# Down products of two SwiGLU blocks: seven block products in place of the plain product, with their sums formed on POOL and kept in DRAM

## The chip, the cores and the metric

The kernel runs on one core of a Trainium2 chip. The metric is the device time of one execution in microseconds (us). Engines: PE multiplies matrices, DVE, ACT and POOL work on elements, and SP issues the DMAs. Each engine has an in-order queue; the order in it is set when the program is built, by a list scheduler of the framework that the kernel is written in.

## The reference

One step of a one-layer streaming encoder on 1024 prompt rows and 64 sample rows of width 1024, in float32, with D_FF = 2816:

```python
def swiglu(x, w_gate, w_up, w_down):
    return (jax.nn.silu(x @ w_gate) * (x @ w_up)) @ w_down

def macaron_half(x, g, b, w_gate, w_up, w_down):
    return layer_norm(ALPHA * x + 0.5 * swiglu(x, w_gate, w_up, w_down), g, b)
```

The layer is `macaron_half`, then a mixer (input projection, sparse attention with an indexer in one group of heads, forgetting attention in the other, output projection, layer norm), then a second `macaron_half`. Keys and values of the new rows are outputs too.

## The kernel before

Each float32 operand is split into a high part (a cast to fp32r on ACT) and a low part (the rest, by a subtraction on DVE; `split`, L106 to L108). A product is then three matmuls of 128x512: high by high, high by low, low by high (`mm`, L111).

**Gate and up** (`ffn_a`). The hidden rows are taken in two halves, j and j + 11, with j from 0 to 10, and the tokens in two halves of 512, so that each of the two weights and the tokens are 2x2 blocks. A body (j, u), u = 0 for gate and 1 for up, forms the block of the product by seven block products (Strassen and Winograd). Its weight sums S1 to S4 come from four POOL operations (L323), with a cast (L326) and a split (L327) of each; its token sums T1 to T4 are formed once, in the stage's start (`finish`), by POOL and DVE. The first product that reads a sum is fy, T2 by S2. The stage's start, j = 0, works without S sums. After body (j, 1) `times` forms the hidden block on DVE (L247) and `emit_h` writes its four blocks of 128x512 to DRAM (L241). The blocks live in a ring of tiles. Gate and up weights are loaded two bodies ahead (`raw_of`, L411).

**Down** (`ffn_b`, `gemm_b`). Plain: three groups of three token tiles, 22 k-steps each. A k-step loads 128x1024 of `w_down` (L202) and the tokens of the group (L487), splits both, and multiplies: eight token tiles need 3 matmuls for each 512 columns, and the ninth tile, the 64 sample rows with their low parts beside them, needs 2. The weights are read three times. Then come residual, layer norm (`layer_norm`, L499 to L519) and the turned operand for the next stage.

The order of the kernel is `ffn_a` and `ffn_b` of the first block, the mixer, the output projection, and `ffn_a` and `ffn_b` of the second block. All loads and stores go through SP's queue. Names that the rows use: gb for the accumulators of the down product, fa, fy, fz and fs for those of gate and up, wst for a raw weight tile, ringz0 and ringz1 for tiles of the ring, zz for residual rows, hd for the hidden blocks in DRAM.

Of the kernel before, what the change touches and what calls it, by code (L numbers as in the profile page):

```python
# [18 lines left out]
P = 128  # L19
# [27 lines left out]
def hybrid_step(ctx: ExitStack, tc: tile.TileContext, i, o):  # L47
# [70 lines left out]

    def turned(t, z, hf):
        r = rows_of(t)  # L120
        pt = sm(f"xt{t}_{hf}")
# [92 lines left out]
    def ffn_a(xo, wg, wu, hd, during, tags, pre=()):  # L214
# [153 lines left out]
        def sample(j, pss):  # L368
# [12 lines left out]
            for b in range(2):  # L381
                DMA.dma_start(hd[j + b * NJ][:, SEQ:TT], hs[:, b * DEC:(b + 1) * DEC])
# [112 lines left out]
    def layer_norm(t, z, acc, gt, bt):  # L495
# [6 lines left out]
        yield  # L502
        st = sp.tile([P, 2, 6], F32, tag="bst", name="bst")
# [60 lines left out]

    def ffn_b(hd, wd, gn, bn, res, emit, last=False):
        with tc.tile_pool(name="hb", bufs=1) as hb_:
            st = {}

            def room(late):
                if late == 0:  # L570
                    st["room"] = hb_.tile([P, 4, 2, 1024], F32R, tag="room", name="room")
                return st["room"][:, late, 0, :], st["room"][:, late, 1, :]

            gemm_b(NF, h_split(hd, st), wd, zz_pre(st, res, gn, bn), zz_post(st, emit), 1, 4, room, last)

    hd1 = [dp.tile([P, TT], F32, name=f"hd1_{k}") for k in range(NF)]
    hd2 = [dp.tile([P, TT], F32, name=f"hd2_{k}") for k in range(NF)]
# [104 lines left out]
    with tc.tile_pool(name="xe", bufs=1) as xe:  # L682
        xo = Strassen(xe)
        ring_of(xo, ("z1",))
        wg1, wu1 = w2("ffn1_w_gate"), w2("ffn1_w_up")
        ffn_a(xo, wg1, wu1, hd1, cgen, ("z0",), load_x(xo, wg1, wu1))
# [17 lines left out]
    ap_ = tc.tile_pool(name="att", bufs=1)  # L704
# [21 lines left out]
    pin_ = tc.tile_pool(name="pin", bufs=1)  # L726
# [77 lines left out]
    def in_proj(gi, tiles=range(NT), ahead=2):  # L804
# [3 lines left out]
        for t in tiles:  # L808
# [10 lines left out]
            pump((0, 0, 3, 3, 0, 0, 0, 0, 0)[t] if gi == 0 else 3)  # L819
# [50 lines left out]
    pidx_ = tc.tile_pool(name="pidx", bufs=1)  # L870
# [351 lines left out]
    in_proj(0, range(2, 6))  # L1222
    cached_kidx()
    in_proj(1, range(6), -1)
    pump_all()
    in_proj(0, range(6, NT), -1)
    in_proj(1, range(6, NT), 7)
# [10 lines left out]
    pc_ = tc.tile_pool(name="pc", bufs=2)  # L1238
# [348 lines left out]
    pf_ = tc.tile_pool(name="pf", bufs=2)  # L1587
# [30 lines left out]
    xe_ = tc.tile_pool(name="xe2", bufs=1)  # L1618
# [27 lines left out]
    ffn_a(xo2[0], w2("ffn2_w_gate"), w2("ffn2_w_up"), hd2, iter(()), ("z1", "z0"))  # L1646
# [58 lines left out]
```

## Time and profile before

| | |
|---|---|
| median of 3 runs | 2414.56 us (2414.2 to 2414.74) |
| profiled execution, its own time | 2413.24 us |
| its span | 2411.5 us |
| PE busy | 2275.1 us (94%), 11999 matmuls |
| DVE busy | 1571.4 us (65%) |
| ACT busy | 1058.9 us (44%) |
| POOL busy | 743.3 us (31%) |
| DMA | 316.4 MB, 131 GB/s on average |
| chain that ended last | PE 76%, DVE 14%, DMA 3%, issue 3%, ACT 3%, POOL 1% |

The stages lie, in us of the span, at 0 to 519 (gate and up, first block), 519 to 792 (down), 792 to 1535 (mixer), 1535 to 1640 (output projection), 1640 to 2137 (gate and up, second block, with its start to 1705) and 2137 to the end (down). A share over the whole span mixes them, so the windows of a stage say more. A wait is named by what ended it. PEclk is the granted share of PE's full clock.

### The profile page before, as it was taken

To read this page: it belongs to the slowest core of one execution; us is meant where nothing else is said; L and a number is where in the kernel's file an instruction comes from. 1 tells how busy PE (TensorE), PEld (TensorE's weight loads), DVE (VectorE), ACT (ScalarE), POOL (GpSimd) and SP (SyncE) were. 2 spreads that over 40 slices of the span, in tenths; PEclk is the share of its full clock that TensorE was granted. 3 is DMA by queue.
4 is the path that set the end of the run, shared out by engine and by line. 5 is a ranking of instruction groups with operands and counts; after the bars stand their busy time and mean duration, and the time that the engine had idled before them with its cause. 6 is when DMAs were issued, how large, how long until landed. Compare 5 with 4: busy or idle time off the path is not lost.

```text
span 2411.5 us, 34602 instructions
## 1 busy us (share of the span) xinstructions
PE 2275.1 (94%) x11999; PEld 1936.8 (80%) x11999; DVE 1571.4 (65%) x2680; ACT 1058.9 (44%) x1999; POOL 743.3 (31%) x1018
## 2 busy tenths in 40 slices
PE   8899999999999999887778999999899999999997
PEld 6788888888887999787667887788688888888885
DVE  7555465544665545999988777588754655545665
ACT  4333333333444356664556788633333333333432
POOL 4322232200001434225367677503432322200010
PEclk9999999999999999998878999999999999999999
DMA  4444432256666344243366741553132222265673
GB/s 156 141 140 133 121 91 64 80 175 191 198 196 213 102 133 148 76 135 101 92 149 152 189 115 43 166 187 111 56 95 63 89 64 80 80 204 169 211 225 113
DMA packets 293625, 316.42 MB, mean 131 GB/s; under 512 B 41326, under 2 KB 241454, under 8 KB 293450
## 3 DMA queue, kind: packets, MB, share of 16 engines
q1 hardware_dynamic: 293450, 314.20, 43.3%
q8 instruction: 95, 1.56, 0.3%
q14 instruction: 80, 0.66, 0.1%
HBM read 235.54 MB, written 78.58 MB: 130 GB/s over the span
## 4 chain that ended last, share of the span: by engine, by line
PE 76%; DVE 14%; DMA 3%; issue 3%; ACT 3%; POOL 1%; SPq 0%; DVEq 0%; POOLq 0%; ACTq 0%
PE fa L111 20%; PE gb L111 16%; PE fz L111 9%; PE fy L111 5%; PE ip L111 5%; DVE s L984 4%; PE gb_a L111 4%; PE gb_b L111 4%; PE fs L111 3%; PE pq L111 2%; PE acc L111 2%; PE pt L1406 2%; PE iq L111 1%; PE xt L124 1%; DMA wst<-ffn_w_down 1%
## 5 line engine op out<-in xcount | busy, mean ns | idle before, releaser
L107 ACT CAST wh<-wst 128x1024 fp32r<-128x1024 f32 x232 | 244.0, 1052 | 348.8 <-PE fs L111 144.5
L108 DVE TENSOR_TENSOR wl<-wst,wh 128x1024 fp32r<-128x1024 f32 x232 | 294.5, 1270 | 133.8 <-ACT wh L107 130.3
L326 ACT CAST Sh<-S 128x512 fp32r<-128x512 f32 x160 | 97.0, 619 | 238.8 <-PE fa L111 148.8
L323 POOL TENSOR_TENSOR S<-wst 128x512 f32<-128x512 f32 x80 | 109.4, 1368 | 273.4 <-DVE Sl L327 147.5
L490 POOL CAST hh<-hl 128x64 fp32r<-128x64 f32 x36 | 19.6, 545 | 537.9 <-DVE hl L108 528.2
L327 DVE TENSOR_TENSOR Sl<-S,Sh 128x512 fp32r<-128x512 f32 x160 | 150.5, 944 | 23.7 <-ACT Sh L326 22.5
L111 PE MATMUL gb<-wh,hh 128*128 128x512 f32 x480 | 154.3, 392 | 5.8 <-ACT hh L107 5.8
L323 POOL TENSOR_TENSOR S<-wst,S 128x512 f32<-128x512 f32 x40 | 72.0, 1799 | 249.5 <-issue 155.6
L107 ACT CAST hh<-hr 128x384 fp32r<-128x384 f32 (+1 forms) x120 | 59.7, 497 | 200.3 <-PE gb_b L111 167.2
L111 PE MATMUL gb<-wl,hh 128*128 128x512 f32 x480 | 146.1, 389 | 0.0
L108 DVE TENSOR_TENSOR hl<-hr,hh 128x384 fp32r<-128x384 f32 (+1 forms) x120 | 64.3, 535 | 124.1 <-ACT hh L107 114.3
L111 PE MATMUL gb<-wh,hl 128*128 128x512 f32 x480 | 140.4, 389 | 0.0
L111 PE MATMUL acc<-pp,vs 128*128 128x256 f32 (+1 forms) x640 | 122.9, 311 | 7.2 <-DVE pp L108 5.0
L108 DVE TENSOR_TENSOR pp<-pt,pp 128x512 fp32r<-128x512 f32 (+1 forms) x160 | 98.0, 630 | 21.0 <-ACT pp L107 20.4
L1362 POOL TENSOR_SCALAR e<-e,su 128x128 f32<-128x128 f32 (+7 forms) x128 | 99.8, 791 | 33.7 <-DVE su L1359 17.8
L111 PEld LDWEIGHTS gb<-wh,hh 128*128 128x128 f32 x480 | 89.0, 188 | 25.4 <-ACT hh L107 7.5
L111 PE MATMUL ip<-wh,xh 128*128 128x256 f32 x368 | 107.6, 292 | 1.7 <-DVE lt L659 1.6
L111 PEld LDWEIGHTS acc<-pp,vs 128*128 128x128 f32 x640 | 96.9, 204 | 14.9 <-DVE pp L108 8.6
L1406 PE MATMUL pt<-ident,e 128*128 128x128 f32 x576 | 99.8, 294 | 9.2 <-POOL e L1362 8.5
L991 ACT ACTIVATE csum<-s,neg 128x1024 f16<-128x1024 f32 (+1 forms) x62 | 72.9, 1175 | 80.7 <-DVE neg L988 77.8
L111 PE MATMUL ip<-wh,xl 128*128 128x256 f32 x368 | 105.6, 287 | 0.0
L111 PE MATMUL ip<-wl,xh 128*128 128x256 f32 x368 | 105.5, 287 | 0.0
(496 smaller groups left out, 7028.0 us busy)
## 6 DMA issues: line engine op xcount, KB each, us to landing
wst<-ffn_w_down SPq DMA_DIRECT2D x132, 512.0 KB
wst<-ffn_w_gate SPq DMA_DIRECT2D x88, 256.0 KB
wst<-ffn_w_up SPq DMA_DIRECT2D x88, 256.0 KB
hd<-ringz SPq DMA_DIRECT2D x88, 256.0 KB
hr<-hd SPq DMA_DIRECT2D x88, 192.0 KB
wst<-w_out SPq DMA_DIRECT2D x24, 512.0 KB
hr<-hd SPq DMA_DIRECT2D x44, 160.0 KB
wst<-w_in SPq DMA_DIRECT2D x12, 512.0 KB
```

The source lines that it names most:

```text
L107: S.copy(hi, src)
L108: V.tensor_tensor(lo, src, f(hi), ALU.subtract)
L111: PE.matmul(out, lhsT, rhs, start=start, stop=stop, skip_group_check=more)
L124: PE.transpose(pt[:, q * r:(q + 1) * r], z[:r, k * P:(k + 1) * P], ident[:r, :r])
L323: G.tensor_tensor(t, ss[0] if x is None else x, ss[1] if y is None else y, op)
L326: S.copy(hi, t)
L327: V.tensor_tensor(lo, t, f(hi), ALU.subtract)
L490: G.tensor_copy(hh[:, 320:384], f(hl[:, 256:320]))
L984: V.tensor_scalar(junk.bitcast(src.dtype)[:, :n], src[:, of:of + n], th[:, e:e + 1], None, op, ALU.add, accum_out=out[:, e:e + 1])
L991: S.activation(csum[:, :n], sc[b], AF.Sign, bias=neg[:, e:e + 1], scale=1.0, accum_out=cnt[:, e:e + 1])
L1362: G.tensor_scalar(es[q][:, :n], es[q][:, :n], su2[:, q:q + 1], 1.0, ALU.mult, ALU.mult)
L1406: PE.transpose(pt[:, m * P:(m + 1) * P], e[:, kt * P:(kt + 1) * P], ident)
```

## The change

- `ffn_b` is new. The down product is taken as 2x2 blocks of tokens (512 each), hidden rows and output columns (512 each), by seven block products P1 to P7, each of 4 token tiles x 11 k x 3 matmuls. A step is a pair of k. The sample rows need the plain blocks of `w_down`, and B12 is in none of the seven, so a step list `OPS` holds it as an entry of its own, with sample matmuls alone. Operands are loaded two steps ahead into tiles of three buffers; each product keeps its last two pairs (three in P4) to finish tile by tile.
- `emit_h` writes seven blocks for each j in place of four: A11, A12, A22 and the sums S1 to S4, formed by four POOL operations.
- `emit_w`, called at the end of each j, loads both 128-row slices of `w_down` of that j into one tile w4, forms T1 to T4 in it by four POOL operations, and writes them to DRAM. w4 has one buffer.
- The long-lived pools are placed at one end of SBUF and the stages' pools at the other, with waits by tile (`reuse_waits="tile"`) where a stage's pool follows another in the same room.
- The input projection's first two column groups are taken in another order of token tiles, and the turned tiles take a larger PSUM tile while the down product runs.

```diff
-    cst = ctx.enter_context(tc.tile_pool(name="cst", bufs=1))
-    xpool = ctx.enter_context(tc.tile_pool(name="xp", bufs=1))
-    wp = ctx.enter_context(tc.tile_pool(name="wp", bufs=3))
-    mp = ctx.enter_context(tc.tile_pool(name="mp", bufs=2))
-    zp = ctx.enter_context(tc.tile_pool(name="zp", bufs=1))
-    sp = ctx.enter_context(tc.tile_pool(name="sp", bufs=4))
+    cst = ctx.enter_context(tc.tile_pool(name="cst", bufs=1, side="left"))
+    xpool = ctx.enter_context(tc.tile_pool(name="xp", bufs=1, side="left"))
+    zp = ctx.enter_context(tc.tile_pool(name="zp", bufs=1, side="right"))
+    mp = ctx.enter_context(tc.tile_pool(name="mp", bufs=2, side="right"))
+    sp = ctx.enter_context(tc.tile_pool(name="sp", bufs=4, side="right"))
+    wp = ctx.enter_context(tc.tile_pool(name="wp", bufs=3, side="right"))
...
         def emit_h(j, keep):
-            for ff, c0, c in ((j, 0, keep[0]), (j + NJ, 512, keep[1]), (j + NJ, 0, keep[2]), (j, 512, keep[3])):
-                DMA.dma_start(hd[ff][:, c0:c0 + 512], c)
+            a11, a22, a12, a21 = keep
+            s1, s2, s4 = (xo.tmp() for _ in range(3))
+            G.tensor_tensor(s1, a21, a22, ALU.add)
+            G.tensor_tensor(s2, s1, a11, ALU.subtract)
+            G.tensor_tensor(a21, a11, a21, ALU.subtract)
+            G.tensor_tensor(s4, a12, s2, ALU.subtract)
+            for nm, c in (("A11", a11), ("A12", a12), ("A22", a22), ("S1", s1), ("S2", s2), ("S3", a21), ("S4", s4)):
+                DMA.dma_start(hd[nm][j // 2][j % 2], c)
...
+        def emit_w(j):
+            w4 = zp.tile([P, 4, 512], F32, tag="z2", name="w4")
+            for r in range(2):
+                DMA.dma_start(w4[:, 2 * r:2 * r + 2, :].rearrange("p a c -> p (a c)"),
+                              wd[(j + r * NJ) * P:(j + r * NJ + 1) * P, :])
+            b11, b12, b21, b22 = (w4[:, q, :] for q in range(4))
+            G.tensor_tensor(b11, b12, b11, ALU.subtract)
+            G.tensor_tensor(b12, b22, b12, ALU.subtract)
+            G.tensor_tensor(b22, b22, b11, ALU.subtract)
+            G.tensor_tensor(b21, b21, b22, ALU.subtract)
+            for nm, c in (("T1", b11), ("T3", b12), ("T2", b22), ("T4", b21)):
+                DMA.dma_start(hd[nm][j // 2][j % 2], c)
...
             next(late[-1])
+            emit_w(j)
...
+    PAIRS = [(k, min(2, NJ - k)) for k in range(0, NJ, 2)]
+    OPS = {"P1": ("A11", "B11"), "B12": (None, "B12"), "P2": ("A12", "B21"), "P3": ("S4", "B22"), "P6": ("S2", "T2"),
+           "P5": ("S1", "T1"), "P7": ("S3", "T3"), "P4": ("A22", "T4")}
...
-            gemm_b(NF, h_split(hd, st), wd, zz_pre(st, res, gn, bn), zz_post(st, emit), 1, 4, room, last)
...
+        with tc.tile_pool(name="hb", bufs=1, side="left", reuse_waits="tile") as hb_:
+            zt = {}
...
+            def fetch(src, n, tg):
+                st = wp.tile([P, 1024], F32, tag=tg, name="raw")
+                DMA.dma_start(st[:, :n * 512].rearrange("p (k c) -> p k c", k=n), src)
+                return st
+
+            def load(i):
+                if i >= len(steps):
+                    return
+                p, q = steps[i]
+                A, B = OPS[p]
+                n = PAIRS[q][1]
+                raws = [(fetch(w_src(B, q), n, "st"), "mh", "ml")]
+                if A is not None:
+                    raws.append((fetch(hd[A][q][0:n].rearrange("k p c -> p k c"), n, "wl"), "lh", "ll"))
+                out = []
+                for st, th, tl in raws:
+                    h_, l_ = (hb_.tile([P, 1024], F32R, tag=tg, name=tg, bufs=3) for tg in (th, tl))
+                    split(h_[:, :n * 512], l_[:, :n * 512], st[:, :n * 512])
+                    out += [h_.rearrange("p (k c) -> p k c", k=2), l_.rearrange("p (k c) -> p k c", k=2)]
+                ops[i] = out
...
+            def product(acc, t, i, first, stop):
+                wh, wl, hh, hl = ops[i]
+                n = PAIRS[steps[i][1]][1]
+                cs = slice(t * P, t * P + P)
+                for k in range(n):
+                    mm(acc, hh[:, k, cs], wh[:, k, :], first and k == 0, False)
+                    mm(acc, hh[:, k, cs], wl[:, k, :], False, False)
+                    mm(acc, hl[:, k, cs], wh[:, k, :], False, stop and k == n - 1)
...
+            def evict(p, t, acc):
+                if p == "P1":
+                    u.append(mp.tile([P, 512], F32, tag="ssum", name=f"u{t}", bufs=4))
+                    S.copy(u[t], acc)
+                    begin(t, 0, acc)
+                elif p == "P2":
+                    add(t, 0, acc)
+                elif p == "P3":
+                    begin(t, 1, acc)
+                elif p == "P6":
+                    V.tensor_tensor(u[t], acc, u[t], ALU.add)
+                    add(t, 1, u[t], G)
+                elif p == "P5":
+                    add(t, 1, acc)
+                    begin(t + 4, 1, acc)
+                    todo.extend([finish(t)] * 6)
+                elif p == "P7":
+                    V.tensor_tensor(u[t], acc, u[t], ALU.add)
+                    add(t + 4, 1, u[t], G)
+                    begin(t + 4, 0, u[t])
+                else:
+                    add(t + 4, 0, acc)
+                    g = finish(t + 4)
+                    if last:
+                        for _ in g:
+                            pass
+                    else:
+                        todo.extend([g] * 6)
...
+            for p in OPS:
+                late = 3 if p == "P4" else 2
+                acc = [sm(f"fb{p}_{t}") for t in range(4)] if p != "B12" else None
+                if p == "P2":
+                    load_s(1)
+                d = {"P1": 0, "B12": 1, "P2": 0, "P3": 1}.get(p)
+                for q in range(len(PAIRS)):
+                    load(i + q + 2)
+                    if i + q == 2:
+                        blocks(hold)
+                    if acc is not None and q < len(PAIRS) - late:
+                        for t in range(4):
+                            product(acc[t], t, i + q, q == 0, False)
+                    if d is not None:
+                        wh, wl = ops[i + q][:2]
+                        for k in range(PAIRS[q][1]):
+                            ks = PAIRS[q][0] + k
+                            for w in (wh, wl):
+                                mm(samp[:, d * 512:(d + 1) * 512], hold["hs"][:, ks, :], w[:, k, :],
+                                   p in ("P1", "B12") and ks == 0 and w is wh, p in ("P2", "P3") and ks == NJ - 1 and w is wl)
+                    pump(3)
+                if acc is not None:
+                    if p == "P4":
+                        pump_all()
+                    for t in range(4):
+                        for q in range(len(PAIRS) - late, len(PAIRS)):
+                            product(acc[t], t, i + q, False, q == len(PAIRS) - 1)
+                        evict(p, t, acc[t])
...
-    pidx_ = tc.tile_pool(name="pidx", bufs=1)
+    pidx_ = tc.tile_pool(name="pidx", bufs=1, side="left", reuse_waits="tile")
```

The list scheduler orders the new work. Second FFN, POOL, before: the weight sums of body (4,0), S1_18260 on, directly follow those of body (3,1).

```order
L323 TENSOR_TENSOR S4_18118<-wst_18095,S2_18110 128x512
L323 TENSOR_TENSOR S1_18260<-wst_18246,wst_18249 128x512
L323 TENSOR_TENSOR S2_18264<-S1_18260,wst_18246 128x512
L323 TENSOR_TENSOR S3_18268<-wst_18246 128x512
L323 TENSOR_TENSOR S4_18272<-wst_18249,S2_18264 128x512
L323 TENSOR_TENSOR S1_18410<-wst_18396,wst_18399 128x512
```

In the change, the same sums (S1_18280 on) with what stands ahead of them; each w4 is one `emit_w`:

```order
L260 TENSOR_TENSOR w4_19859<-w4_19859 128x512
L257 TENSOR_TENSOR w4_20180<-w4_20180 128x512
L258 TENSOR_TENSOR w4_20180<-w4_20180 128x512
L259 TENSOR_TENSOR w4_20180<-w4_20180 128x512
L260 TENSOR_TENSOR w4_20180<-w4_20180 128x512
L257 TENSOR_TENSOR w4_20501<-w4_20501 128x512
L258 TENSOR_TENSOR w4_20501<-w4_20501 128x512
L259 TENSOR_TENSOR w4_20501<-w4_20501 128x512
L260 TENSOR_TENSOR w4_20501<-w4_20501 128x512
L344 TENSOR_TENSOR S1_18280<-wst_18266,wst_18269 128x512
L344 TENSOR_TENSOR S2_18284<-S1_18280,wst_18266 128x512
```

All eleven `emit_w` of the block stand ahead of the sums of (4,0) now. The same place in SP's queue, before; wst_18246 and wst_18249 are the weights of those sums, and hd2 is the hidden block:

```order
L241 DMA hd2_2_122<-ringz1_17157 128x512
L411 DMA wst_18095<-ffn2_w_up 128x4x128 x2
L411 DMA wst_18246<-ffn2_w_gate 128x4x128 x2
L241 DMA hd2_13_133<-ringz1_17157 128x512 x2
L411 DMA wst_18249<-ffn2_w_gate 128x4x128 x2
L241 DMA hd2_2_122<-ringz1_17157 128x512
```

In the change, the last two w4 (hd1A11_1_166 between them is the A11 of j = 3; the weights wst_18266 and wst_18269 stand some 15 and 20 rows ahead):

```order
L254 DMA w4_20180<-ffn2_w_down 128x1024 x2
L262 DMA hd1T1_4_211<-w4_20180 128x512
L262 DMA hd1T3_4_223<-w4_20180 128x512
L262 DMA hd1T2_4_217<-w4_20180 128x512
L262 DMA hd1T4_4_229<-w4_20180 128x512
L249 DMA hd1A11_1_166<-ringz0_17109 128x512
L254 DMA w4_20501<-ffn2_w_down 128x1024 x2
L262 DMA hd1T1_5_212<-w4_20501 128x512
L262 DMA hd1T3_5_224<-w4_20501 128x512
L249 DMA hd1A22_1_178<-ringz0_17109 128x512
L262 DMA hd1T2_5_218<-w4_20501 128x512
L262 DMA hd1T4_5_230<-w4_20501 128x512
```

A load of a w4 waits for the writes of the one before it, and the last stands behind the write of A11 of j = 3. The start of the second gate/up stage, POOL, before (S1_17348 is the first body's sum; L186 to L194 belong to `finish`):

```order
L191 TENSOR_TENSOR ringz0_17158<-ringz0_17158,B11h_16088 128x512
L194 TENSOR_TENSOR ringz0_17158<-B21h_16090,ringz0_17158 128x512
L323 TENSOR_TENSOR S1_17348<-wst_17334,wst_17337 128x512
L323 TENSOR_TENSOR S2_17352<-S1_17348,wst_17334 128x512
L197 TENSOR_TENSOR T4l_16095<-ringz0_17158,T4h_16094 128x4x128
```

In the change (L188 to L199 belong to `finish`, S1_17317 is the first body's sum):

```order
L257 TENSOR_TENSOR w4_17612<-w4_17612 128x512
L188 TENSOR_TENSOR ringz0_17109<-B22h_16043,T1h_16721 128x512
L199 TENSOR_TENSOR T4l_16046<-ringz0_17109,T4h_16045 128x4x128
L258 TENSOR_TENSOR w4_17612<-w4_17612 128x512
L193 TENSOR_TENSOR ringz0_17109<-ringz0_17109,B11h_16039 128x512
L196 TENSOR_TENSOR ringz0_17109<-B21h_16041,ringz0_17109 128x512
L344 TENSOR_TENSOR S1_17317<-wst_17303,wst_17306 128x512
L259 TENSOR_TENSOR w4_17612<-w4_17612 128x512
L193 TENSOR_TENSOR ringz0_17109<-ringz0_17109,B11h_16039 128x512
L196 TENSOR_TENSOR ringz0_17109<-B21h_16041,ringz0_17109 128x512
L344 TENSOR_TENSOR S2_17321<-S1_17317,wst_17303 128x512
L344 TENSOR_TENSOR S3_17325<-wst_17303 128x512
```

Operations on w4 stand between those of `finish` and ahead of the first sums.

## Rows read from the trace of the kernel before

**Rows 1.** Windows by stage: length, busy us (instructions) per engine, granted clock, DMA share, GB/s.

```profile
519.50:792.00 272.50, 269.81 (x1211) 222.17 (x1209) 163.05 (x237) 105.74 (x153) 12.19 (x22) 1.00 0.64 201
1705.00:2127.00 422.00, 418.03 (x1955) 344.80 (x1956) 231.88 (x274) 133.93 (x206) 116.27 (x80) 0.99 0.25 78
2137.00:2400.00 263.00, 258.60 (x1137) 212.82 (x1135) 151.04 (x222) 96.06 (x136) 12.03 (x22) 1.00 0.61 195
2400.00:2411.50 11.50, 0.00 (x0) 0.00 (x0) 7.58 (x18) 0.20 (x1) 0.00 (x0) 0.64 0.33 114
```

**Rows 2.** Chain of waits, first down product and second gate/up stage: start, us, what.

```profile
600.77 2.72 PE gb L111 x12
...
1905.72 2.79 PE fa L111 x12
```

**Rows 3.** Waits of PE, first and second down product: us, times, longest.

```profile
PE gb L111 <- ACT hh L107: 2.7, 2, 2.0
...
PE gb L111 <- ACT hh L107: 3.1, 2, 1.6
```

**Rows 4.** Chain of waits, first down product, a 512 KB load.

```profile
757.55 4.92 DMA wst<-ffn_w_down
```

**Rows 5.** Groups of POOL, second gate/up stage: busy us, mean ns; idle before.

```profile
L323 POOL TENSOR_TENSOR S<-wst 128x512 f32<-128x512 f32 x37 | 48.3, 1307 | 106.7 <-DVE Sl L327 103.8 <-DMA wst<-ffn_w_gate 2.3
L323 POOL TENSOR_TENSOR S<-wst,S 128x512 f32<-128x512 f32 x19 | 31.8, 1675 | 144.1 <-issue 82.4 <-DMA wst<-ffn_w_up 61.7
```

**Rows 6.** Chain of waits, first gate/up stage, a 256 KB write.

```profile
73.94 3.52 DMA hd<-ringz
```

**Rows 7.** Timeline of SP, second gate/up stage: start, us, what.

```profile
1737.42 0.32 SPq L241 DMA_DIRECT2D hd<-ringz  x1
```

**Rows 8.** DMA view of 1737 to 1741, 40 slices: busy share in tenths.

```profile
DMA  0000000000004999999300000000000000000000
```

**Rows 9.** Chain of waits, start of the second gate/up stage.

```profile
1706.07 1.68 POOL S L323
```

**Rows 10.** Waits of PE, 1700 to 1712.

```profile
PE fy L111 <- ACT Sh L326: 7.4, 1, 7.4
```

**Rows 11.** Window behind that wait (columns as in rows 1).

```profile
1705.00:1710.00 5.00, 1.03 (x3) 0.85 (x4) 4.86 (x4) 1.14 (x2) 5.00 (x4) 0.50 0.33 104
```

**Rows 12.** Timelines of POOL, DVE, SP and PE around body (4,0), second FFN.

```profile
1806.37 1.29 POOL L323 TENSOR_TENSOR S<-S,wst 128x512 f32<-128x512 f32 x1 [2.69 <-issue]
...
1822.32 0.69 DVE L247 SCALAR_TENSOR_TENSOR ringz<-ringz,fa 128x512 f32<-128x512 f32 x1 [4.30 <-PE fa L111]
...
1823.04 0.32 SPq L241 DMA_DIRECT2D hd<-ringz  x1
...
1832.85 0.39 PE L111 MATMUL fy<-T2h,Sh 128*128 128x512 f32 x1
```

**Rows 13.** Timelines of DVE, POOL and ACT, the same place.

```profile
1827.51 0.69 DVE L327 TENSOR_TENSOR Sl<-S,Sh 128x512 fp32r<-128x512 f32 x1
...
1829.69 1.57 DVE L327 TENSOR_TENSOR Sl<-S,Sh 128x512 fp32r<-128x512 f32 x1
...
1829.43 1.29 POOL L323 TENSOR_TENSOR S<-wst 128x512 f32<-128x512 f32 x1
...
1828.91 0.62 ACT L326 CAST Sh<-S 128x512 fp32r<-128x512 f32 x1 [0.92 <-PE fa L111]
```

**Rows 14.** Groups of DVE, first down product (columns as in rows 5).

```profile
L108 DVE TENSOR_TENSOR wl<-wst,wh 128x1024 fp32r<-128x1024 f32 x60 | 73.5, 1225 | 31.6 <-ACT wh L107 31.0 <-DMA zz<-x_prompt 0.5
L517 DVE SCALAR_TENSOR_TENSOR zz<-zz,bmv,gb 128x1024 f32<-128x1024 f32 x7 | 8.9, 1274 | 0.0
L507 DVE BATCH_NORM_STATS2 bst<-zz 128x6 f32<-128x512 f32 x14 | 8.9, 668 | 0.0
L499 DVE SCALAR_TENSOR_TENSOR zz<-zz,gb 128x512 f32<-128x512 f32 x10 | 6.3, 680 | 1.3 <-PE gb L111 1.3
```

**Rows 15.** Chain of waits at the pool change of the mixer.

```profile
1208.07 0.27 SPq L1309
```

More of the change, by code (lines that the diff above doesn't have):

```diff
@@ L380, in sample @@
             S.copy(hs[:, 0:P], pt[:, 0:P])
-            for b in range(2):
-                DMA.dma_start(hd[j + b * NJ][:, SEQ:TT], hs[:, b * DEC:(b + 1) * DEC])
+            DMA.dma_start(hd["s"].rearrange("r p j c -> p j r c")[:, j], hs[:, 0:P].rearrange("p (r c) -> p r c", r=2))
             yield
@@ L502, in layer_norm, with ln_tail @@
         yield
+        yield from ln_tail(t, z, gt, bt)
+    def ln_tail(t, z, gt, bt):
+        r = rows_of(t)
         st = sp.tile([P, 2, 6], F32, tag="bst", name="bst")
@@ L576, in hybrid_step, with blocks, w_src, load_s @@
-    hd1 = [dp.tile([P, TT], F32, name=f"hd1_{k}") for k in range(NF)]
-    hd2 = [dp.tile([P, TT], F32, name=f"hd2_{k}") for k in range(NF)]
+        wide_[0] = True
+        with tc.tile_pool(name="hb", bufs=1, side="left", reuse_waits="tile") as hb_:
+            zt = {}
+            def blocks(hold):
+                for t0, pool, tg in ((0, hb_, "z3"), (3, zp, "z0"), (6, zp, "z1")):
+                    z3 = pool.tile([P, 3, D], F32, tag=tg, name="zz")
+                    for t in range(t0, t0 + 3):
+                        zt[t] = z3[:, t - t0, :]
+                        DMA.dma_start(zt[t][:rows_of(t)], res(t)[:rows_of(t)])
+                hold["gb"] = zp.tile([P, 2, D], F32, tag="z2", name="gb")
+                load_gb(hold["gb"][:, 0, :], hold["gb"][:, 1, :], gn, bn)
+            hold = {}
+            steps = [(p, q) for p in OPS for q in range(len(PAIRS))]
+            ops = {}
+            def w_src(nm, q):
+                k0, n = PAIRS[q]
+                if nm[0] == "T":
+                    return hd[nm][q][0:n].rearrange("k p c -> p k c")
+                r, c = int(nm[1]) - 1, int(nm[2]) - 1
+                return wd[(r * NJ + k0) * P:(r * NJ + k0 + n) * P, c * 512:(c + 1) * 512].rearrange("(k p) c -> p k c", p=P)
+            def fetch(src, n, tg):
[17 more added lines that the diff above has]
+                ops[i] = out
+            def load_s(r):
+                raw = xpool.tile([P, KD, P], F32, tag="xs", name="hsr", bufs=2).rearrange(
+                    "p k c -> p (k c)")[:, 0:NJ * DEC].rearrange("p (k c) -> p k c", k=NJ)
+                DMA.dma_start(raw, hd["s"][r])
+                hs = hb_.tile([P, NJ, P], F32R, tag="hs", name="hs2")
+                split(hs[:, :, 0:DEC], hs[:, :, DEC:P], raw)
+                hold["hs"] = hs
+            def product(acc, t, i, first, stop):
[6 more added lines that the diff above has]
+                    mm(acc, hl[:, k, cs], wh[:, k, :], False, stop and k == n - 1)
+            u = []
+            def z_of(t, d):
+                return zt[t][:, d * 512:(d + 1) * 512]
+            def begin(t, d, acc):
+                V.scalar_tensor_tensor(z_of(t, d), z_of(t, d), ALPHA, acc, ALU.mult, ALU.add)
+            def add(t, d, acc, eng=V):
+                eng.tensor_tensor(z_of(t, d), acc, z_of(t, d), ALU.add)
+            def finish(t):
+                yield from ln_tail(t, zt[t], hold["gb"][:, 0, :], hold["gb"][:, 1, :])
+                yield from emit(t, zt[t])
+            def evict(p, t, acc):
[26 more added lines that the diff above has]
+                        todo.extend([g] * 6)
+            load_s(0)
+            load(0)
+            load(1)
+            samp = big("fbs")
+            i = 0
+            for p in OPS:
[26 more added lines that the diff above has]
+                        evict(p, t, acc[t])
+                if p == "P3":
+                    def tail8():
+                        yield from layer_norm(8, zt[8], (samp[:, 0:512], samp[:, 512:1024]),
+                                              hold["gb"][:, 0, :], hold["gb"][:, 1, :])
+                        yield from emit(8, zt[8])
+                    todo.extend([tail8()] * 7)
+                i += len(PAIRS)
@@ L579, in load_x @@
+        wide_[0] = False
+    hds = []
+    for n in range(2):
+        hd_ = {nm: [dp.tile([2, P, 512], F32, name=f"hd{n}{nm}_{q}") for q in range(len(PAIRS))]
+               for nm in ("A11", "A12", "A22", "S1", "S2", "S3", "S4", "T1", "T2", "T3", "T4")}
+        hd_["s"] = dp.tile([2, P, NJ, DEC], F32, name=f"hd{n}s")
+        hds.append(hd_)
+    hd1, hd2 = hds
     def load_x(xo, wg, wu):
@@ L680, in hybrid_step @@
     cgen = cached_all()
-    with tc.tile_pool(name="xe", bufs=1) as xe:
+    with tc.tile_pool(name="xe", bufs=1, side="left", reuse_waits="tile") as xe:
         xo = Strassen(xe)
@@ L1617, in hybrid_step @@
     st2 = {}
-    xe_ = tc.tile_pool(name="xe2", bufs=1)
+    xe_ = tc.tile_pool(name="xe2", bufs=1, side="left", reuse_waits="tile")
     xe = xe_.__enter__()
```

33 lines of the change are left out of this document (14 added, 19 removed).

## The prediction

> **What bounds the kernel now.** I read the windows by stage first [rows 1]. TensorE (PE) is busy for 269.8 of 272.5 us in the first down product, 258.6 of 263 in the second and 418.0 of 422 in the steady part of the second gate/up stage. So those stages are worth what their matmuls cost, plus the few microseconds in which PE waits. Next the chain of waits: it runs through PE from one matmul to the next, twelve of 128x512 in 2.72 us in the down product (0.2267 us each) and twelve in 2.79 us in the gate/up stage (0.2325 each) [rows 2]. Then PE's waits: the first down product loses 2.7 us and the second 3.1 us, both to a cast that comes late [rows 3]. At the end of the program PE has nothing from 2400 on, and VectorE (DVE) closes the run with layer norms [rows 1].
>
> The profiled execution took 2413.24 us, 1.74 more than its span of 2411.5, and lies 1.3 us under the median of the three runs, 2414.56. My sum is made against 2413.24. A run of this kernel can tell 0.2%, some 4.8 us, from no change.
>
> **Removed: 264 matmuls.** Each down product had 22 k-steps of 52 matmuls, 1144; now it has 7 products x 4 tiles x 11 k x 3 = 924, and 88 for the sample rows: 1012. At 0.2267 us the 264 fewer are 59.8 us. If the new products run at the gate/up stage's 0.2325, the 2024 that remain cost 11.7 us more, which leaves 48. The new operands change as often as the gate/up stage's do, but one accumulator row serves a whole k, as now, so I take a third of that loss: **-56** (-48 to -60).
>
> **Added on POOL: the weight sums.** Each of the 11 `emit_w` of an FFN has one buffer, w4. So its cycle is serial: load two slices of 512 KB at once (one such load took 4.92 us [rows 4]), four 128x512 operations (1.31 to 1.68 us each [rows 5]; I take 1.4, so 5.6), then the last of four 256 KB writes to DRAM before the next load may start. One such write held the chain for 3.52 us [rows 6]; another, undisturbed, was issued at 1737.42 [rows 7] and its packets ended near 1739.0, in the 21st of 40 slices of 0.1 us from 1737 on [rows 8]. With 2.2 for the write and 0.7 for issues the cycle is 4.9 + 5.6 + 2.2 + 0.7 = 13.4 us (12.1 with the shortest of each, 15.8 with the longest). POOL and SP run in order, so what stands behind a cycle waits for it. Two places matter.
>
> *Startup.* Now the chain passes POOL's S sum of the first body at 1706.07 [rows 9], and PE's fy product has waited 7.4 us for the cast of it [rows 10]; PE's granted clock is 0.50 in that stretch, which is the lower level, 1.2 GHz [rows 11]. In the change seven w operations stand ahead of that S2 in the second FFN, eight ahead of its like in the first. Some fall into gaps before the finish operations; five on the path at 1.4 us are 7. I take **+8 and +7** (3 to 12 each).
>
> *S sums of j = 4.* Today POOL makes S2 of body (4,0) at 1806.37, over 26 us before PE's fy reads it at 1832.85 [rows 12]: that lead hides all of POOL. In the change all eleven cycles stand ahead of these S sums, and SP issues the last load behind the write of A11 of j = 3. DVE makes that block at 1822.32 and its write goes out at 1823.04 [rows 12]. From there: load to 1828.3, four operations to 1833.9 (half a us sooner if the first starts on half the load), S1 and S2 at 1.4 us to 1836.2, cast and split of 0.62 and 0.69 [rows 13] to 1837.5. PE comes there 12 matmuls later than now, at 1835.6. So it waits 1 to 2 us, or 4 with operations of 1.68 us, and the emit_h sums and S sums in between push it on. I take 4 for S of (4,0) and 1 for (3,0), **+10** over both FFNs (0 to 36).
>
> *Clock.* After each of these waits some 5 us run at half clock, where a matmul takes twice as long [rows 11]. Two places already pay this; I add **+5** (2 to 10).
>
> The emit_h sums, four POOL operations a j, and three more writes of 256 KB are hidden: POOL has 116 of 422 us in this stage and 88 more operations of 1.4 us bring it to 239; the DMA share is 0.25 [rows 1]. If that cover goes, it goes at the S sums above.
>
> Here the operations meet DVE. A DVE split takes 0.69 us alone and 1.57 with a POOL operation beside it [rows 13], and POOL's own group means are 1.31 to 1.68 [rows 5]. The Trainium skill, page "SBUF — State Buffer", section "Who interferes with whom", says that DVE and GpSimd share a port pair as an exclusive lock: a DVE operation with two SBUF inputs and a GpSimd operation block each other for the whole instruction. The 1.57 agrees with it. By that rule, taken for every operation, each w sum would also be held for one split, 1.31 + 0.69 = 2.0 us, the cycle would be 15.8 us as in the second rival and the sum 2431; the rows' means lie nearer to 1.4.
>
> **Changed in the down product.** Between P1 and P2 stands B12, for the sample rows alone: 22 matmuls, 5 us, for 2.75 MB of weights, with 1 MB for P2 behind. P1's tail (36 matmuls) and B12 give 13.2 us of cover. The stage moves 201 GB/s at a DMA share of 0.64 [rows 1], so 3.75 MB take 12 us at full share, 19 at today's rate, and then come a cast and a split of 1.23 [rows 14]. That is 1 to 8 us late; I take 5 in each FFN, **+10**. At the change from P7 to P4 DVE has eight evictions of 0.68, four layer norms of some 4.9 us (two statistics of 0.67, two products of 1.27, small ones [rows 14]) and the splits, near 33 us against 30 us of PE: **+4** for both, with **+2** for the clock after B12. Today's waits of 2.7 and 3.1 go: **-5.8**. At the end four tiles close one by one on 15 matmuls (3.4 us) each against 4.9 us on DVE, so the last ends about 9.4 us after PE, plus the write; now 11.5 us pass in all [rows 1]: **+3** (0 to 6). Together +13 (5 to 25).
>
> **Pools.** At the pool change in the mixer the load of vs went out at 1208.07, held by all earlier transfers [rows 15]. In the change it waits for fewer of them, while it stays behind the last kaT write: **-1.5** (-6 to +4). The other stages keep their order.
>
> Sum: -56 - 1.5 + 15 + 10 + 5 + 13 = -14.5, so **2399 us**.
>
> **The rivals.**
> 1. *The gain is kept whole* (0.17). For it: POOL is busy for little over a quarter of the time, and the S sums have 26 us of lead. Against it: the sums are queued serially. Startup 6, no wait at (4,0), clock 2, down products 5: -44.5, about 2369 (2362 to 2384).
> 2. *The weight-sum chain paces the gate/up stage* (0.26). Mechanism: one buffer, so load, four POOL operations and write follow each other, and the S sums stand behind. It decides from a cycle of about 15 us. At 15.8, with three cycles after the last point of slack, S of (4,0) comes 7 to 10 us later, the startup 5 later, in each FFN, with 4 for the clock: +32, **2431** (2418 to 2445), slower than before. For it: the longest rows of each part give just that. Against it: their means don't.
> 3. *The down product is paced by its loads and DVE* (0.15). Every product needs new operands on both sides. If each of six changeovers costs the 2.7 us of [rows 3], that is 16 us an FFN, in one or in both: 2415 to 2431. Against it: DVE has 163 of 272 us there, and ACT 106 [rows 1].
> That the matmuls are not fewer can be left out: the instruction streams show 264 less.
>
> **Numbers.** My forecast holds 0.42, its own range 2385 to 2412. Faster by over 0.2%: 0.35 of the forecast, rival 1 whole and 0.02 of rival 3, 0.54. Within 0.2%: 0.07 + 0.04 + 0.05, 0.16. Slower: 0.22 of rival 2 and 0.08 of rival 3, 0.30. The range takes in most of rivals 1 and 2: 2370 to 2436.
>
> **What would show it.** Right: 11737 matmuls; about 245 us for each down product; a first wait of PE for Sh a few us above 7.4, and one near 4 us for Sh of body (4,0); a PE gap of 5 us between P1 and P2. Wrong: w cycles under 12 us and no wait at (4,0) (rival 1); a w cycle over 15 us with waits of 10 us and more in the steady gate/up stage (rival 2); PE waiting for mh or lh splits at each change of product (rival 3); a matmul interval in the down products above 0.233 us.

## The result and the profile after

The changed kernel takes 2426.24 us (median of 7 runs, 2421.51 to 2431.46), the kernel before 2413.64 beside it (7 runs, 2409.76 to 2414.74). The ratio is 1.0055, with a 95% interval of 1.0041 to 1.0069: slower by half a per cent, where 2399 was forecast. The time lies in the stated range; the direction was forecast wrongly, and the second rival (the weight-sum chain, 2418 to 2445) is what came.

The profiled execution took 2428.18 us with a span of 2426.4, 14.9 more than the span before. The stages, from the first matmul of each to that of the next (starts read from the tiles' views of both kernels, to 0.1 us):

| stage | before | after | difference |
|---|---|---|---|
| gate and up, first block | 519.8 | 555.0 | +35.2 |
| down, first block | 272.0 | 244.6 | -27.4 |
| mixer | 744.0 | 742.2 | -1.8 |
| output projection | 104.2 | 106.7 | +2.5 |
| gate and up, second block | 491.8 | 522.2 | +30.4 |
| down, second block, to the end | 279.7 | 255.7 | -24.0 |

By these starts the down products give 51.4 us and the gate/up stages take 65.6. The boundary is not quite the same in both kernels: before, the last twelve matmuls of each gate/up stage, 2.8 us, stand behind the first eight of the down product, and in the change none do. So the gain is nearer to 46 us and the loss nearer to 60.

First the windows of the changed kernel that answer to [rows 1]: the down product of the first block, the second block's gate and up from 1745 to 1880 and from there on, the second down product, and the end.

```profile
555.00:799.50 244.50, 239.46 (x1052) 194.88 (x1053) 164.11 (x204) 94.56 (x114) 22.79 (x13) 0.99 0.64 211
1745.00:1880.00 135.00, 119.20 (x526) 96.88 (x525) 76.47 (x76) 34.52 (x53) 100.22 (x67) 0.94 0.64 216
1880.00:2170.00 290.00, 289.81 (x1372) 241.20 (x1370) 158.88 (x187) 90.11 (x140) 116.35 (x77) 1.00 0.31 97
2170.70:2410.00 239.30, 233.36 (x1008) 189.58 (x1009) 156.91 (x193) 87.61 (x102) 21.78 (x12) 0.99 0.62 205
2411.00:2426.40 15.40, 0.09 (x1) 0.00 (x0) 11.57 (x31) 0.41 (x2) 0.00 (x0) 0.62 0.34 136
```

The second gate/up stage has two parts. From 1880 on PE is full, 289.8 of 290 us, with the hidden-block sums on POOL and their writes still running. Up to 1880 PE lacks 16 of 135 us, its clock is 0.94, POOL is busy for 100 us and the DMA share is 0.64. The eleventh emit_w ends in it, at 1867.

The first block loses in the same part. The next two rows run from the first fy of body (1,0) to that of (4,0), before and after:

```profile
82.00:220.00 138.00, 136.66 (x637) 112.38 (x638) 74.95 (x107) 48.12 (x84) 39.47 (x25) 0.98 0.43 131
86.00:249.00 163.00, 144.79 (x637) 115.93 (x637) 95.56 (x103) 46.66 (x80) 106.19 (x71) 0.93 0.72 236
```

The same 637 matmuls take 25 us more. In 17 of these PE is idle, and 8 are longer matmuls at the lower clock, 0.93 in place of 0.98.

The chain of waits in the first down product, which answers to [rows 2] (rows left out at the dots, and the short issue rows in all chains below):

```profile
561.78 11.79 PE fbP L111 x52
...
595.78 0.68 DVE zz L663
596.46 2.28 DVE ml L108 x2
598.75 4.00 DMA raw<-ffn_w_down
602.86 1.05 ACT mh L107
603.95 7.00 PE fbP L111 x26
```

Before the break 52 matmuls take 11.79 us, 0.2267 each: the interval of the old product, not that of gate and up. The break is B12: its operands come late, and the chain goes through DVE's splits to a load of 4.00 us. P2 starts at 603.95, with 26 matmuls in 7.00 us (0.269 each), a part of them at half clock. PE is not idle all that time: B12's own sample matmuls run in it, with waits of 3.3 us in all.

The waits of PE in the second gate/up stage, which answer to [rows 10]:

```profile
PE fz L111 <- DVE ringz L370: 8.6, 2, 4.3
PE fa L111 <- ACT ringz L357: 7.9, 1, 7.9
PE fy L111 <- ACT Sh L347: 4.8, 2, 3.2
```

The second row is the wait of the stage's start, which the kernel before had as a wait of fy. The other two are new. Row one is DVE's eviction L370 into a ring tile, which is not free yet. DVE's and SP's waits from 1740 to 1880 and to 1870 say for what:

```profile
DVE ringz L370 <- DMA hd1S<-ringz: 16.0, 2, 10.0
SPq L262 <- POOL w L259: 11.3, 9, 3.5
```

The ring tile waits for the write of a hidden-block sum to DRAM. That write stands in SP's queue among the transfers of emit_w, and there the writes L262 wait for POOL's operations: 40.9 us in all four rows of this kind, of which the row shown is the longest. By these rows SP's in-order queue passes POOL's delay on to the ring. In the first block the waits of PE are mostly at the S sums: up to the first fy of (4,0), 7.3 us for Sh and 4.6 for Sl.

POOL's own waits, between 1720 and 1870, say why. Before:

```profile
POOL S L323 <- issue: 42.8, 7, 16.8
POOL S L323 <- DVE Sl L327: 41.1, 10, 6.6
```

After:

```profile
POOL w L257 <- DMA w<-ffn_w_down: 24.4, 4, 6.3
POOL w L257 <- issue: 3.5, 2, 3.3
```

Before, POOL idles for 42.8 us at the S sums for no releaser that the profile shows: that was their lead. After, no such time is left at the S sums; POOL idles for loads of w4.

The chain itself, from the fourth w4 and, below, from the tenth to the first fy of body (4,0):

```profile
1760.01 1.30 POOL w L260
1761.33 2.10 DMA hd1T<-w
1763.45 3.56 DMA w<-ffn_w_down
1767.04 1.32 POOL S L344
1769.91 1.75 POOL w L257
...
1781.47 1.72 POOL w L260
1783.21 3.91 DMA hd1T<-w
...
1853.38 1.30 POOL w L260
1854.70 2.01 DMA hd1T<-w
1856.79 3.59 DMA w<-ffn_w_down
1860.54 1.30 POOL w L257
1861.91 1.31 POOL w L258
1863.29 1.62 POOL w L259
1864.99 2.16 POOL w L260
1867.15 1.23 POOL S L344
1868.45 1.27 POOL S L344
1869.74 0.63 ACT Sh L347
```

```profile
1870.41 0.50 PE L111 MATMUL fy<-T2h,Sh 128*128 128x512 f32 x1 [3.23 <-ACT Sh L347]
```

L260 is the last operation of a w4, hd1T its write, w the load of the next. The nine L260 from 1747.16 to 1864.99 lie on the chain, 14.7 us apart on average (117.8 / 8). The last two are 11.6 apart: 2.0 for the write, 3.6 for the loads, 6.0 for four operations and what lies between. The one at 1781.47 came 21.5 after its predecessor, because five S sums and an emit_h sum stand before and between its four operations. POOL does not wait there: it is busy for 19.4 of the 19.5 us from 1763.5 to 1783, and one of these sums takes 4.40 us. In the eight cycles POOL forms 16 S sums and 8 emit_h sums, 40 us of work. The loads on the chain differ too: 3.6 us on four turns, 4.1 to 6.2 on three. The S sums of (4,0) run at 1867.15, and fy at 1870.41. Measured from the start of the stage that is 221.9 us, against 192.9 before, so 29.0 late. Behind it come one wait of 0.85 us for a split and some matmuls at half clock; from 1880 on PE is full.

### The profile page after: what moved, and what is told of

It reads as the page before. It is cut to its first block, busy times and chain, and to the rows that moved or that the text cites. A ratio compares the mean times of both kernels' runs of the same rounds, so it can differ in the third digit from the quotient of the medians.

```text
span 2426.4 us, 34202 instructions
## 1 busy us (share of the span) xinstructions
PE 2232.1 (92%) x11735; PEld 1893.7 (78%) x11735; DVE 1641.7 (68%) x2640; ACT 1038.2 (43%) x1927; POOL 1019.6 (42%) x1166
## 4 chain that ended last, share of the span: by engine, by line
PE 58%; DVE 18%; DMA 8%; POOL 6%; issue 4%; ACT 4%; SPq 1%; POOLq 0%; DVEq 0%; ACTq 0%
PE fbP L111 15%; PE fa L111 12%; PE fz L111 6%; PE ip L111 5%; DVE s L1157 4%; PE fy L111 3%; DMA w<-ffn_w_down 3%; PE gb L111 3%; PE fs L111 2%; PE pq L111 2%; PE acc L111 2%; PE pt L1579 1%; PE fbs L111 1%; PE iq L111 1%; POOL S L344 1%
## 5 line engine op out<-in xcount | busy, mean ns | idle before, releaser
L111 PE MATMUL fbP<-ml,lh 128*128 128x512 f32 x616 | 238.5, 391 | 1.6 <-DVE ml L108 1.6
L111 PE MATMUL fbP<-mh,ll 128*128 128x512 f32 x616 | 237.9, 390 | 2.1 <-DVE ll L108 2.1
L107 ACT CAST wh<-wst 128x1024 fp32r<-128x1024 f32 x108 | 113.0, 1050 | 277.7 <-PE fs L111 112.2
L111 PE MATMUL fbP<-mh,lh 128*128 128x512 f32 x616 | 228.0, 392 | 2.7 <-ACT lh L107 1.7
L108 DVE TENSOR_TENSOR wl<-wst,wh 128x1024 fp32r<-128x1024 f32 x108 | 152.8, 1417 | 75.0 <-ACT wh L107 73.3
L108 DVE TENSOR_TENSOR ll<-raw,lh 128x1024 fp32r<-128x1024 f32 x84 | 99.9, 1189 | 114.2 <-ACT lh L107 110.9
L111 PEld LDWEIGHTS fbP<-mh,lh 128*128 128x128 f32 x616 | 115.8, 189 | 27.9 <-ACT mh L107 2.1
L111 PEld LDWEIGHTS fbP<-ml,lh 128*128 128x128 f32 x616 | 115.6, 188 | 28.0 <-DVE ml L108 4.2
L111 PEld LDWEIGHTS fbP<-mh,ll 128*128 128x128 f32 x616 | 115.7, 188 | 26.8 <-DVE ll L108 2.9
L108 DVE TENSOR_TENSOR ml<-raw,mh 128x1024 fp32r<-128x1024 f32 x96 | 116.4, 1218 | 11.0 <-ACT mh L107 9.4
```

The source lines that it names most:

```text
L107: S.copy(hi, src)
L108: V.tensor_tensor(lo, src, f(hi), ALU.subtract)
L111: PE.matmul(out, lhsT, rhs, start=start, stop=stop, skip_group_check=more)
```

## The experiments

Theory A: the order costs the time. POOL's in-order queue holds the S sums (and the emit_h sums, which free ring tiles) behind a serial chain of load, four operations and write, eleven times in the first four and a half j of each block. Rivals: the added work and traffic cost it wherever they stand (B), or the start of the stage alone does (C). A kernel's gate/up stages are given as in the table above (555.0 and 522.2 in the change). A time without a number of runs is one run.

### One emit_w per j

```diff
-                G.tensor_tensor(t, ss[0] if x is None else x, ss[1] if y is None else y, op)
+                last_s[:] = [G.tensor_tensor(t, ss[0] if x is None else x, ss[1] if y is None else y, op).ins]
...
-            emit_w(j)
+            for n in [j - 1][:j] + [j][:j // (NJ - 1)]:
+                with tc.issue_after(last_s[0]):
+                    emit_w(n)
```

> Each emit_w is kept behind the last S sum of its own j on POOL (one cycle per j, over all eleven j), nothing else changes: the same operations, loads and writes. Theory A (POOL's in-order queue holds the S sums and the emit_h sums behind the serial weight-sum cycles): the two gate/up stages, 555 and 522 us in the changed kernel, fall to about 525 and 500, the waits of PE for Sh and for ring tiles go, and the time is 2370 to 2388. Rival B (the added POOL operations and 58 MB of DMA cost the time wherever they stand): no change, 2420 to 2430. Rival C (the start alone is at fault, where DVE meets POOL): about 15 us less, 2405 to 2415.

Measured: 2366.17 us (4 runs, 2364.08 to 2367.16), 0.9815 of the kernel before (0.9784 to 0.9847). The stages are 522.7 and 490.8. With the same operations and bytes, 60 us of the change's time are gone, a little more than the range I gave for A. Rivals B and C fall, A stands. The edge both puts emit_w behind the S sums and spreads it over all j; which of the two counts comes below. The windows of the second gate/up stage:

```profile
1710.00:1845.00 135.00, 135.00 (x646) 112.85 (x645) 75.03 (x88) 41.86 (x64) 72.63 (x48) 1.00 0.45 148
1845.00:2104.00 259.00, 259.00 (x1227) 215.83 (x1225) 150.90 (x170) 81.71 (x127) 146.83 (x97) 1.00 0.46 151
```

PE has no idle time in either. POOL's waits from 1684 to 1840:

```profile
POOL S L344 <- issue: 35.0, 3, 14.0
POOL S L344 <- DVE Sl L348: 9.6, 4, 5.8
```

Its slack at the S sums is back, 35.0 us.

### Without the weight sums

```diff
-                if nm[0] == "T":
-                    return hd[nm][q][0:n].rearrange("k p c -> p k c")
-                r, c = int(nm[1]) - 1, int(nm[2]) - 1
+                r, c = (0, 0) if nm[0] == "T" else (int(nm[1]) - 1, int(nm[2]) - 1)
...
-            emit_w(j)
```

> Left out: the sums T1 to T4 with their loads and writes; the products that use them read a plain block of w_down of the same size. Theory A: about the time of the paced kernel or a little less, 2365 to 2385, since pacing hides what is left out here. Rival B: well below the paced kernel, near 2375 where the paced one stays at 2425. If the seven products gain nothing by themselves: above 2405.

Measured: 2357.72 us, under the range, with stages of 518.7 and 490.8. The whole of emit_w costs 68.5 us in the change and 8.5 paced. So pacing hides nearly all of it, in the second block all. The sums of emit_h are still formed here, and cost these stages nothing.

### Loads and writes without the operations

```diff
-            G.tensor_tensor(b11, b12, b11, ALU.subtract)
-            G.tensor_tensor(b12, b22, b12, ALU.subtract)
-            G.tensor_tensor(b22, b22, b11, ALU.subtract)
-            G.tensor_tensor(b21, b21, b22, ALU.subtract)
```

> Left out: the four POOL operations of each emit_w; the loads into the one buffer and the writes from it stay, in their order. Theory A (POOL's queue is what is held): most of the loss goes, 2370 to 2390. Rival C2 (SP's queue and the DMA traffic hold the gate and up loads): most of it stays, 2405 to 2425.

Measured: 2379.64 us, stages of 532.0 and 498.7. Of the 68.5 us, 46.6 go with POOL's operations and 21.9 stay with the transfers as the change orders them. PE's waits in the first block:

```profile
PE fa L111 <- ACT wh L107: 11.5, 2, 9.5
PE fy L111 <- ACT Sh L343: 2.3, 2, 2.0
```

What stays is mostly another wait: PE for the cast of a gate or up weight, whose load stands in SP's queue.

### Without the sums of the hidden blocks

```diff
-            s1, s2, s4 = (xo.tmp() for _ in range(3))
-            G.tensor_tensor(s1, a21, a22, ALU.add)
-            G.tensor_tensor(s2, s1, a11, ALU.subtract)
-            G.tensor_tensor(a21, a11, a21, ALU.subtract)
-            G.tensor_tensor(s4, a12, s2, ALU.subtract)
+            s1, s2, s4 = a11, a22, a12
```

> Left out: the four POOL operations of each emit_h; seven blocks are still written, S1, S2 and S4 from A11, A22 and A12, so that three ring tiles less are in use. Theory A: the ring waits (16 us of PE in the second block and what they bring of half clock) go at least in part, since the ring is freed without POOL, but the waits for Sh stay: 2400 to 2415. Rival (the ring waits have another cause, the writes): 2420 to 2430.

Measured: 2416.84 us, just above the first range; stages of 545.9 and 515.3, so 9 and 7 us less than the change. (Its last down product is 9.5 us longer, so the whole gains less.) That is a quarter of the gate/up loss, though the same sums cost nothing where emit_w is left out: they cost beside emit_w. The run doesn't tell their ring tiles from their POOL time. The 16 us that I called ring waits of PE are DVE's; PE's own are 8.6.

### The first two emit_w early

```diff
-            for n in [j - 1][:j] + [j][:j // (NJ - 1)]:
-                with tc.issue_after(last_s[0]):
-                    emit_w(n)
+            if j < 2:
+                emit_w(j)
+            else:
+                with tc.issue_after(last_s[0]):
+                    emit_w(j)
```

> The paced kernel, but the first two emit_w of each block go back to where the change has them, in the stage's start; the other nine stay behind the S sums of their own j. Theory A says that the start is the smaller share: the first fy of the second block starts near 77 us into its stage (77.6 in the change, 68.6 paced) and the time is 2366 plus 10 to 20, 2376 to 2386. Rival C (the start is at fault): 2400 or more.

Measured: 2375.21 us, at the lower edge; the first fy of the second block starts 77.5 us into its stage, as in the change (paced 68.6, before 69.0). The start is worth about 9 us in all, and C falls for the rest.

### Two emit_w per j

```diff
-            for n in [j - 1][:j] + [j][:j // (NJ - 1)]:
+            for n in range(max(0, 2 * j - 2), min(NJ, 2 * j)):
```

> Paced, but two emit_w behind the S sums of each j from 1 to 6, so that all are done after six j in place of eleven (the change has them done after four and a half). Two cycles of 11.3 us or more stand against a lead of some 26 us of the S sums. Theory A: a small loss that starts where S and emit_h sums share the room, 2368 to 2385; above 2400 it would say that the density alone makes the loss, not the place ahead of the S sums.

Measured: 2393.32 us, outside what I gave: the second stage loses 5 us to the paced one (495.9), as expected, but the first 28 (550.5). So the place behind an S sum isn't enough in the first block; how many come per j matters there. Two runs were made on the cause.

*The same with POOL issuing the transfers* (`DMA.dma_start` becomes `G.dma_start` in emit_w):

> Two emit_w per j as before, but their loads and writes are issued by POOL in place of SP. In the kernel with SP the first block lost 28 us (gate/up 550 against 523 paced), the second 5, and the chain there ran through SP to the casts of gate and up weights. Theory A2 (in the first block SP's queue is held too, by loads that wait for writes and writes that wait for POOL): the first block falls to 522 to 535 and the time to 2365 to 2380. Rival (POOL alone is held, or the traffic is too dense): no change, 2388 to 2398, or more since POOL now waits for its own writes.

Measured: 2405.73 us, the first stage again 550.5, the second 507.6. With SP's queue freed of emit_w's transfers nothing comes back. That speaks against A2, but doesn't rule it out: POOL now waits for its own writes before it issues a load (10.9 us from 80 to 300), and the profile lists POOL's transfers under another DMA queue, q0 (software_dynamic), so the move has a price of its own.

*The same without the four operations, the transfers on SP*, placed behind the gate/up load issued last before them:

> Two emit_w per j with their loads and writes on SP, behind the gate and up loads of their j, and without the four POOL operations each (left out). With POOL operations two per j lost 28 us in the first gate/up stage (550 against 523), and the same 550 with POOL issuing the transfers. If POOL's share is what is lost: the stage ends near 520 to 530 and the time is 2360 to 2372. If the traffic alone does it: the stage ends near 540 to 550 and the time is 2383 to 2395.

Measured: 2358.35 us, just under the range, the first stage 520.8. The windows of 120 to 300 with the operations, and then without:

```profile
120.00:300.00 180.00, 167.40 (x758) 135.91 (x757) 103.38 (x123) 55.84 (x96) 110.93 (x76) 0.94 0.67 219
```

```profile
120.00:300.00 180.00, 178.32 (x853) 147.27 (x852) 101.67 (x137) 63.32 (x109) 70.79 (x49) 1.00 0.76 247
```

Without them PE does 853 matmuls in place of 758, at a higher DMA rate (247 against 219 GB/s). So the traffic at that density is borne, and the loss comes with POOL's operations; the edge that paces the two kernels is not the same (an S sum there, a load here), so a part may be its. Nor do SP's writes wait for POOL here, so the run doesn't tell POOL's time from what it holds up in SP's queue. The first block's gate/up stage also turns the cached keys and values; whether that is why the second block bears two per j and the first doesn't was not tried.

### Another engine, another queue

The paced kernel with the operations of emit_w on DVE (`G.tensor_tensor` becomes `V.tensor_tensor`, behind the last split of the S sums):

> Paced as before, but the four operations of each emit_w run on DVE behind the last split of the S sums of their j. Theory A: whichever engine has room does, since the order no longer holds anything up; DVE takes 0.69 to 1.7 us for such an operation: 2358 to 2375. If DVE is tight in the gate/up stages (its splits feed PE): 2375 to 2395, with waits of PE for wl or Sl.

Measured: 2378.18 us. Its gate/up stages are those of the paced kernel (524.6 and 490.8), so DVE has the room there; the 12 us lie behind them: 4.1 in the first down product, 4.8 in the last, and 3.3 in the mixer, which takes 737.4 to 743.1 us in the profiles of the kernels that share it, so that the 3.3 are within its spread. One new wait of PE, at the first sample operand of the first down product (3.7 us in the last):

```profile
PE fbs L111 <- DVE hs L108: 4.0, 1, 4.0
```

The change with emit_w's transfers issued by POOL:

> The change with the loads and writes of emit_w issued by POOL, nothing paced. Theory A2: SP's share of the loss goes, which the kernel without the POOL operations put at 13 us in the first block and 8 in the second; POOL's share of some 45 stays: 2400 to 2415. If SP had no share: 2420 to 2435.

Measured: 2408.71 us, inside A2's range, with stages of 547.4 and 515.3. But it is weak support, since the move has a price, as the paced kernel shows:

> The paced kernel with the loads and writes of emit_w issued by POOL. The paced kernel is 8 us above the one without weight sums, 4 of them in the first gate/up stage: 2358 to 2368 if that is SP's queue; above 2370 if issuing costs POOL more than it gives back.

Measured: 2380.98 us (4 runs, 2375.96 to 2382.33), 0.9875 of before (0.9859 to 0.9892), 15 us more than with SP. The first stage is shorter by 3.5 us (519.2), which points to SP's queue for what the paced kernel still loses there; the loss lies behind the gate/up stages: 5.6 us in the first down product, 5.9 in the last, and 3.8 in the mixer, within its spread. POOL's timeline shows what an issue takes from POOL:

```profile
311.12 1.09 POOL L254 DMA_DIRECT2D w<-ffn_w_down  x2
```

That is 0.55 us each for the two loads of one w4. In the down products, where emit_w doesn't run, PE waits 2.3 and 1.9 us for the sample operand's split, and 2.5 and 2.6 at one split of a weight. Why these come later is open.

### The pools alone

The kernel before with the `tile_pool` lines of the change (sides, waits by tile), nothing else:

> The kernel before with the pools of the change (ends of SBUF, waits by tile) and nothing else. My sum had -1.5 us for it; the mixer of the changed kernel is 1.8 us shorter, its output projection 2.5 us longer. Expected: within 5 us of the kernel before, 2408 to 2416; a gain of 10 us or more would say that a part of the paced kernel's gain is the pools'.

Measured: 2411.22 us (10 runs), 0.9998 of before (0.9985 to 1.0011). So no gain or loss of the whole comes from the pools alone. They move time between stages: the mixer takes 739.4 us and the output projection 106.7, 4.6 less and 2.5 more than before, the gate/up stages 4.1 and 5.3 less and the down products 4.8 and 5.7 more.

## Why the prediction was wrong

**Removed matmuls: right, too cautious.** The interval stayed at 0.2267 us, so the full 59.8 us, not 56.

**Down product: right in sum.** Forecast -56 + 13 = -43; measured -51.4 by the table, nearer to -46 with the boundary put right. B12 costs PE 3.3 us of waits in the first block and some half clock, where 5 and 1 were forecast; 2.2 more are lost at the start of the stage, which had no term. The change from P7 to P4 costs nothing (39.6 of 40 us busy around it), where 4 were forecast for both blocks. The end is 4 us longer (15.4 with almost nothing on PE in place of 11.5), where 3 were forecast.

**Pools: right in sum**, with no change for them alone. The -1.8 in the mixer against -1.5 is within the mixer's spread. The 2.5 us in the output projection were not foreseen; they come with the pools, whose kernel alone has the same 106.7.

**Startup: right in the second block** (first fy 8.6 us later, 7 forecast), less in the first (3.3 for 8).

**S sums of j = 4: here it failed.** The step reads "I take 4 for S of (4,0) and 1 for (3,0)", +10 over both blocks. Measured from the first fy of the block to that of (4,0), the delay grew by 20.5 us in the second block (29.0 - 8.6) and by 25 in the first (28.6 - 3.3). The wait at (4,0) itself was 3.2 us there and 5.0 in the first, near the 4 that I gave it. The rest came ahead of it, at S sums of earlier bodies, at ring tiles and by the lower clock, for which the sum had next to nothing. The mechanism was named, and its pieces were even too dear: the shortest cycle is 11.6 us, not 13.4 (the two loads take 3.6, not 4.9). What I left out is that other work comes between. POOL also works through S and emit_h sums among the operations of a cycle, so the chain ran at 14.7 us a cycle, close to the 15 that I had called decisive for the second rival. I had tied the last load to the write of A11 of j = 3. That write went out at 1855.07, but it stood behind the four writes of the tenth w4, issued from 1850.61 on: the chain set its time, not DVE. So I summed one place, the last, and let the ten cycles ahead of it be on time.

Of the 68.5 us that emit_w costs in the change, 46.6 go with POOL's operations and 21.9 are the transfers' in that order; 8.5 of the whole stay when it is spread. "POOL has 116 of 422 us" was true, but a mean over the stage hid that all eleven cycles fall into its first 220 us. "If that cover goes, it goes at the S sums" was only half true: in the second block PE's largest new wait, 8.6 us, is at ring tiles that wait for the emit_h writes, which the sum had at nothing.

**Clock: too small.** Forecast +5 for both blocks. The matmuls up to (4,0) alone took some 8 us longer in the first block (144.79 against 136.66 us for 637) and, by an estimate from busy times, 3 in the second (130.1 for 586 against 124.0 for 574, at 0.2267 for each of the 12). [rows 11] lies for four of its five us inside the wait; the price of a wait is in these two windows of the kernel before, behind the first fy at 1709:

```profile
1709.00:1714.00 5.00, 5.00 (x12) 3.65 (x13) 4.93 (x5) 1.12 (x2) 4.37 (x4) 0.53 0.66 194
1714.00:1719.00 5.00, 5.00 (x24) 4.10 (x23) 3.20 (x4) 1.25 (x2) 4.04 (x3) 1.00 0.46 146
```

Twelve matmuls in place of 24 make 2.5 us for each such wait, as the forecast had it; there were more waits. (In [rows 8] the packets end in the 20th slice, not the 21st, which is still 1739.0.)

**Ports.** The rule of exclusive ports gave 2.0 us for each operation and a sum of 2431, near to what came, but not by its means. In the stretch of the chain the operations took

```profile
L257 POOL TENSOR_TENSOR w<-w 128x512 f32<-128x512 f32 x9 | 13.7, 1518 | 27.9 <-DMA w<-ffn_w_down 24.4 <-issue 3.5
L259 POOL TENSOR_TENSOR w<-w 128x512 f32<-128x512 f32 x9 | 14.6, 1624 | 0.5
```

1.5 to 1.6 us on average (before, the means of the S sums were 1.31 and 1.68 [rows 5]). The Trainium skill, page "SBUF — State Buffer", section "Who interferes with whom", calls the port pair an exclusive lock. A mean between 1.31 and 2.0 fits some operations being held and not every one; the S sum of 4.40 us ran beside an unbroken row of DVE operations. The paced kernel, with the same operations beside the same splits, lost nothing in that stage.

## What to carry to other kernels

Work that has room on an engine by its busy share may still cost time, if an in-order queue puts it ahead of work on the path: look where a scheduler put it, and pace it by an edge behind the sums that PE needs next. A chain through one buffer (load, operate, write, load) has to be summed over all its turns, with what stands between them, against the lead of what waits behind it. The paced kernel, with one emit_w per j, beats both: 2366.17 us, 1.85% under the kernel before. A second buffer for w4, which would break the chain in another way, was not tried.

## What the runs showed of the hardware

Two loads of 512 KB at once took 3.6 us from issue to use at the shortest (1856.79 to 1860.40 on the chain) and 6.2 at the longest, where one in the down product took 4.92 [rows 4]. A DMA issue held POOL for 0.55 us. Moving transfers from SP to POOL, which the profile lists under another DMA queue (q0 for q1), made down products 5.6 and 5.9 us longer that have no such transfer; this is not explained. A wait of PE of 7.4 us was followed by 5 us at a granted clock of 0.53, with twelve matmuls in place of 24.
